# A two-matmul MLP on one Trainium2 core: another order of loads at the start, and other engines for the w2 casts and the plain output copies

## The chip, the cores and the metric

The kernel runs on one core of one Trainium2 chip. The time is device microseconds of one execution. Each kernel is executed several times; a time below is the median with the lowest and the highest in brackets.

Names used below: TensorE is PE in the profile (PEld is its weight load), VectorE is DVE, ScalarE is ACT, GpSimd is POOL, SyncE is SP (the engine that issues most of the loads).

## The reference, cut to what matters

```python
# x: 8 x 1024 x 1024, w1: 1024 x 4096, w2: 4096 x 1024, all float32
h = x @ w1
h = 0.5 * h * (1 + np.tanh(np.sqrt(2 / np.pi) * (h + 0.044715 * h ** 3)))   # gelu
return (h @ w2).astype(np.float32)
```

## The kernel before

The 8192 rows of x are worked on in eight superblocks of 1024 rows. The first matmul is done with 7 block products in place of 8: x and w1 are cut into 2 x 2 blocks, and sums of blocks are multiplied. Inputs are float32 in HBM and are cast to float16 on the chip. The first superblock is special. While it runs, w1 and w2 have to be loaded and cast, and the sums are made. Its second matmul is done plainly, in two column halves (`b = 0` and `b = 1`). The second superblock reloads the cast w1 (`raw_d`), makes the sums again and writes them to HBM (`w1_d`, shown as `w_d_77` to `w_d_80` in the profile: the four quarters of w1). From the third superblock on everything is loaded ready made.

Four engines share the small work. Their queues are worked off in order.

The tile pools. `gc` is the float32 staging for loads of weights (4 buffers), `tmp` is the float32 scratch for block results and output tiles (10 buffers), `u` is for all float16 operands.

```python
    up = ctx.enter_context(tc.tile_pool(name="up", bufs=26))
    gcp = ctx.enter_context(tc.tile_pool(name="gcp", bufs=4))
    tp = ctx.enter_context(tc.tile_pool(name="tp", bufs=10))
    # ... (other pools cut)
    def tt(out, in0, in1, op):                      # L107: every VectorE add or subtract
        nc.vector.tensor_tensor(out=out, in0=in0, in1=in1, op=op)
    # ...
    def pool_copy(out, in_):                        # L118: every GpSimd cast
        pool_last[0] = nc.gpsimd.tensor_copy(out=out, in_=in_)
```

The start. `x_first` loads and transposes both halves of x on TensorE; only then are the first columns of w1 loaded.

```python
        if sb == 0:
            quads.append(MadeQuad(0, True))
            xs.make(5)
            cs = quads[0].load_cols(0, 1)
            quads[0].sum(4, cs)
            for m in (1, 3, 7, 6):
                if m != 3:
                    xs.make(m)
                quads[0].sum(m, cs)
            for c, n in ((1, 1), (2, 2)):
                cs = quads[0].load_cols(c, n)
                for m in SUMS:
                    quads[0].sum(m, cs)
        else:
            for step in range(QC):
                ahead(0, step)                      # second superblock: reload raw w1, make sums, write them
```

The sums of the second superblock go to HBM through GpSimd's queue, and so do the output stores:

```python
        def sum(self, m, sl=slice(None)):
            make_sum(self.ops, m, self.raw, KH, QW, sl)
            if not self.first:
                nc.gpsimd.dma_start(out=w1_d[self.q][:, m - 1, :], in_=flat(self.ops[m]))   # L184
        # ...
        def copy_plain(self):
            for m in PLAIN:
                nc.gpsimd.dma_start(out=w1_d[self.q][:, m - 1, :], in_=flat(self.ops[m]))   # L192
    # ...
    def store(sb, b, q, src):
        # ...
        queue = nc.gpsimd if sb < NSB - 1 else nc.sync
        return queue.dma_start(out=out2[r0:r0 + P, o0:o0 + OH], in_=src)                    # L375
```

The second matmul of the first superblock, with its w2 casts and its output copies:

```python
        for b in range(2):
            # ... (eight PSUM banks; mm() is L395)
            for q in range(NI // QC):
                # ...
                        cast_in(
                            raw[f"{a + 1}{b + 1}"][:, j:j + 2, :],
                            w2v[b, a, :, c:c + 2, :],
                            pool_copy if b == 0 and q < 2 else nc.scalar.copy,
                        )
                # ... (matmuls, sums of w2 and their writes)
            for i in range(2 * NQ):
                for c in range(NI - TAIL, NI):
                    mm(i, c, ready[c])
                o = temp()                                  # a tmp buffer
                if i % 2:
                    nc.scalar.copy(out=o, in_=banks[i])
                else:
                    nc.vector.tensor_copy(out=o, in_=banks[i])      # L443
                last = store(sb, f"{i // NQ + 1}{b + 1}", i % NQ, o)
```

In the first matmul of every superblock, four gelus on ScalarE turn a column's results into the blocks g11, g12, g21, g22 (in the profile of before g_215 to g_218).

## Time and profile before

| | before |
|---|---|
| time | 1606.63 us (1605.54 to 1608.92, 3 runs) |
| profiled run: span, mean granted TensorE clock | 1603.7 us, 0.996 |
| TensorE starts: first real matmul / second superblock / its second matmul | 18.28 / 245.73 / 342.60 us |
| from there to the last matmul | 1256.80 us |

TensorE is busy nearly all the time. From the page of before, the first part (busy us, share of the span, instructions) and the chain of waits (shares of the span by engine, then by line):

```profile
PE 1578.2 (98%) x7296; PEld 717.9 (45%) x7296; DVE 819.6 (51%) x1047; ACT 472.3 (29%) x784; POOL 132.1 (8%) x228
...
PE 95%; DMA 3%; DVE 1%; ACT 1%; issue 0%; SPq 0%; POOL 0%; DVEq 0%
```

A full-width matmul takes 0.216 us at full clock, so what can be gained is the idle time of TensorE. These lines are TensorE's order of time in before: start us, duration us, engine, line, operation, operands, how many; then in brackets the idle time just before the group and what ended it.

```profile
34.33 10.17 PE L277 MATMUL ps<-u 128*128 128x512 f16 x46 [0.18 <-DVE tmp L107]
44.65 71.14 PE L277 MATMUL ps<-u 128*128 128x512 f16 x328
123.20 5.97 PE L277 MATMUL ps<-u 128*128 128x512 f16 x20 [7.41 <-ACT g_216 L287]
...
191.68 0.59 PE L395 MATMUL ps<-u,g_217 128*128 128x512 f16 x1 [3.34 <-DVE tmp L443]
...
245.73 97.03 PE L277 MATMUL ps<-u 128*128 128x512 f16 x448
```

The reader sees two waits, 7.41 us for a gelu on ScalarE before the end of the first stage and 3.34 us for an output copy on VectorE between the two column halves. Before 34.33 us there are smaller gaps. From 245.73 us on, the second superblock's first matmul is one row with no wait.

And up to 246 us the DMA engines had no room: their mean busy share ("DMA share") was 1.00 in the first of these two stretches, and 0.70 in the second. In the view by stretches (stretch, length, then busy us and instructions of PE, PEld, DVE, ACT, POOL, then clock, DMA share, GB/s), before:

```profile
185.60:246.00 60.40, 57.06 (x259) 25.53 (x258) 21.06 (x21) 2.37 (x5) 11.92 (x23) 0.97 1.00 382
246.00:342.70 96.70, 96.70 (x449) 43.80 (x448) 64.15 (x89) 45.88 (x80) 12.21 (x24) 1.00 0.70 218
```

### The profile page before, as it was taken

What the parts mean: (1) busy time and instruction counts of PE and PEld (TensorE: products, weight loads), DVE (VectorE), ACT (ScalarE), POOL (GpSimd) and SP (SyncE); (2) the same over time, 40 slices, a digit from 0 to 9 for tenths busy, and PEclk for the clock granted to TensorE, in tenths of its full rate; (3) what the DMA queues carried; (4) which work ended last, traced back from release to release, by engine and by line L of the source; (5) the groups of instructions that cost most, each with busy time, mean ns of one, the idle gap of its engine ahead of it and who ended that gap; (6) DMA issues with size and microseconds to landing.
All of it is one profiled execution on the core that took longest, in us unless ns stands there. A gap on an engine that the chain in (4) does not pass through costs nothing.

```text
span 1603.7 us, 18985 instructions
## 1 busy us (share of the span) xinstructions
PE 1578.2 (98%) x7296; PEld 717.9 (45%) x7296; DVE 819.6 (51%) x1047; ACT 472.3 (29%) x784; POOL 132.1 (8%) x228
## 2 busy tenths in 40 slices
PE   7989999999999999999999999999999999999999
PEld 4434444444444444444444444444444444444444
DVE  6855336644455444555445554456534555455433
ACT  4645104431044210441114410244103431044310
POOL 2230113001100012000120000100001000000000
PEclk9999999999999999999999999999999999999999
DMA  9999998674566646546574565746557464544511
GB/s 306 345 316 361 276 397 280 179 288 146 197 188 184 236 171 228 157 153 262 186 221 144 169 238 197 227 131 226 201 203 246 102 265 158 210 157 178 216 53 53
DMA packets 161820, 338.91 MB, mean 211 GB/s; under 512 B 72257, under 2 KB 78401, under 8 KB 160833
## 3 DMA queue, kind: packets, MB, share of 16 engines
q1 hardware_dynamic: 146944, 278.97, 50.4%
q0 software_dynamic: 14784, 58.73, 11.5%
q8 instruction: 57, 0.93, 0.2%
q14 instruction: 35, 0.28, 0.1%
HBM read 266.34 MB, written 85.98 MB: 220 GB/s over the span
## 4 chain that ended last, share of the span: by engine, by line
PE 95%; DMA 3%; DVE 1%; ACT 1%; issue 0%; SPq 0%; POOL 0%; DVEq 0%
PE ps L277 46%; PE ps L461 42%; PE ps L395 7%; DMA gc<-in_w_dram 2%; DVE u L107 1%; ACT u L137 0%; DVE tmp L107 0%; DMA u<-in_x_dram 0%; DMA u<-xb 0%; SPq L115 0%; POOL u L118 0%; ACT g_218 L287 0%; ACT g_216 L287 0%; ACT g_217 L287 0%; ACT tmp L343 0%
## 5 line engine op out<-in xcount | busy, mean ns | idle before, releaser
L277 PE MATMUL ps<-u 128*128 128x512 f16 x3584 | 779.8, 380 | 13.1 <-ACT g_216 L287 7.7
L107 DVE TENSOR_TENSOR tmp<-tmp,ps 128x512 f32<-128x512 f32 x652 | 447.1, 687 | 661.6 <-PE ps L461 333.3
L277 PEld LDWEIGHTS <-u 128*128 128x128 f16 x3584 | 351.1, 98 | 440.3 <-issue 15.9
L461 PE MATMUL ps<-u,gc 128*128 128x512 f16 x2240 | 485.7, 379 | 0.0
L461 PEld LDWEIGHTS <-gc 128*128 128x128 bf16 x2240 | 219.2, 98 | 264.3
L375 POOL DMA_DIRECT2D out_dram<-tmp x112 | 60.6, 542 | 1108.0 <-ACT tmp L481 733.9
L107 DVE TENSOR_TENSOR u<-u 128x2048 f16<-128x2048 f16 (+2 forms) x110 | 123.0, 1152 | 56.6 <-ACT u L137 21.5
L343 ACT COPY tmp<-ps 128x512 f32<-128x512 f32 x128 | 73.0, 570 | 258.2 <-PE ps L277 258.2
L107 DVE TENSOR_TENSOR tmp<-ps,tmp 128x512 f32<-128x512 f32 x128 | 88.4, 691 | 5.9 <-PE ps L277 1.2
L481 ACT COPY tmp<-ps 128x512 f32<-128x512 f32 x28 | 16.4, 586 | 177.3 <-PE ps L461 177.3
L395 PE MATMUL ps<-u,g_217 128*128 128x512 f16 x128 | 49.0, 383 | 3.3 <-DVE tmp L443 3.3
L395 PE MATMUL ps<-u,g_218 128*128 128x512 f16 x128 | 49.0, 383 | 0.0
L395 PE MATMUL ps<-u,g_215 128*128 128x512 f16 x128 | 48.9, 382 | 0.0
L395 PE MATMUL ps<-u,g_216 128*128 128x512 f16 x128 | 48.8, 381 | 0.0
L137 ACT CAST u<-gc 128x1024 f16<-128x1024 f32 x36 | 37.2, 1044 | 37.6 <-DMA gc<-in_w_dram 37.6
L487 ACT COPY tmp<-ps 128x512 f32<-128x512 f32 x28 | 16.4, 586 | 80.3 <-PE ps L461 80.3
L475 ACT COPY tmp<-ps 128x512 f32<-128x512 f32 x28 | 16.4, 586 | 74.9 <-PE ps L461 74.9
L118 POOL CAST u<-gc 128x1024 f16<-128x1024 f32 (+1 forms) x26 | 28.5, 1105 | 73.8 <-DMA gc<-in_w_dram 60.0
L254 POOL DMA_DIRECT2D xb<-in_x_dram x56 | 27.5, 509 | 18.1 <-DMA out_dram<-tmp 14.5
L441 ACT COPY tmp<-ps 128x512 f32<-128x512 f32 x8 | 4.7, 586 | 71.1 <-PE ps L395 71.1
L395 PEld LDWEIGHTS <-g_218 128*128 128x128 bf16 x128 | 12.6, 98 | 18.8 <-issue 3.9
L395 PEld LDWEIGHTS <-g_215 128*128 128x128 bf16 x128 | 12.6, 99 | 15.5 <-issue 0.8
(120 smaller groups left out, 848.8 us busy)
## 6 DMA issues: line engine op xcount, KB each, us to landing
gc<-in_w_dram SPq DMA_DIRECT2D x64, 512.0 KB, 6.8
out_dram<-tmp POOLq DMA_DIRECT2D x112, 256.0 KB, 4.4
u<-w_d_85 SPq DMA_DIRECT2D x49, 512.0 KB, 6.4
u<-w_d_86 SPq DMA_DIRECT2D x49, 512.0 KB, 7.1
u<-w_d_87 SPq DMA_DIRECT2D x49, 512.0 KB, 5.8
u<-w_d_88 SPq DMA_DIRECT2D x49, 512.0 KB, 6.3
u<-w_d_77 SPq DMA_DIRECT2D x42, 512.0 KB, 4.8
u<-w_d_78 SPq DMA_DIRECT2D x42, 512.0 KB, 5.1
```

Of the source, the lines that this page charges most:

```text
L107: nc.vector.tensor_tensor(out=out, in0=in0, in1=in1, op=op)
L118: pool_last[0] = nc.gpsimd.tensor_copy(out=out, in_=in_)
L137: cast(out=dst, in_=st)
L254: nc.gpsimd.dma_start(out=xb[q:q + P, :], in_=x2[s * SB + q:s * SB + q + P, :])
L277: nc.tensor.matmul(bank, lhsT=ops[m][:, k, cs], rhs=xs[m][:, k, :], start=(first and k == 0), stop=(k == KH - 1), skip_group_check=not first,)
L343: nc.scalar.copy(out=v, in_=pb)
L375: return queue.dma_start(out=out2[r0:r0 + P, o0:o0 + OH], in_=src)
L395: nc.tensor.matmul(banks[i], lhsT=g[f"{i // NQ + 1}{a + 1}"][:, c, (i % NQ) * P:(i % NQ + 1) * P], rhs=w[a], start=(c == 0 and a == 0), st ...
L461: nc.tensor.matmul(banks[q], lhsT=a[:, c, :], rhs=pieces[c // QC][:, c % QC, :], start=(first and c == 0), stop=(c == NI - 1), skip_group_ ...
L475: nc.scalar.copy(out=v[q], in_=ps)
L481: nc.scalar.copy(out=c21, in_=ps)
L487: nc.scalar.copy(out=c12, in_=ps)
```

## The change

Three parts, with the intent of each.

1. Start: the first two column chunks of w1's first column half are loaded between the two halves of x, in two loads of wider rows, so that the first product can follow the transposes at once.
2. Casts: all w2 casts of the first column half go to GpSimd (before: half of them), and of the second column half only the first two quarters stay on ScalarE.
3. Copies: all plain output copies of the first superblock go to ScalarE, so that none stands behind VectorE's subtractions.

```diff
-        def load_cols(self, c, n):
+        def load_cols(self, c, n, b):
             cs = slice(c * P, (c + n) * P)
-            kn = 2 * KH // n
-            for b in range(2):
-                cast = (nc.scalar.copy, pool_copy)[b]
-                for k in range(2 * KH - kn, -1, -kn):
-                    # ... (loads of kn chunks of rows, cast per half)
+            for a in (1, 0):
+                st = gcp.tile([P, KH, n * P], F32, name="gc")
+                load_in_order(st, w1v[b, :, a * KH:(a + 1) * KH, cs])
+                cast = pool_copy if (a, b) == (0, 1) else nc.scalar.copy
+                cast(out=self.raw[f"{a + 1}{b + 1}"][:, :, cs], in_=st)
             return cs
@@ x_first returns a function half(a) that loads and transposes one half of x @@
@@ start of the first superblock @@
-            quads.append(MadeQuad(0, True))
-            xs.make(5)
-            cs = quads[0].load_cols(0, 1)
-            # ... (sums of chunk 0, then loads and sums of chunk 1 and of chunks 2-3)
+            first = MadeQuad(0, True)
+            quads.append(first)
+            x_half(1)
+            xs.make(2)
+            cs = first.load_cols(0, 2, 0)
+            first.sum(4, cs)
+            x_half(0)
+            xs.make(5, 1)
+            first.load_cols(0, 2, 1)
+            first.sum(1, cs)
+            first.sum(3, cs)
+            for m in (7, 6):
+                xs.make(m)
+                first.sum(m, cs)
+            for b in range(2):
+                cs = first.load_cols(2, 2, b)
+            for m in SUMS:
+                first.sum(m, cs)
@@ w2 casts @@
-                            pool_copy if b == 0 and q < 2 else nc.scalar.copy,
+                            nc.scalar.copy if b == 1 and q < 2 else pool_copy,
@@ output copies of the first superblock @@
-                if i % 2:
-                    nc.scalar.copy(out=o, in_=banks[i])
-                else:
-                    nc.vector.tensor_copy(out=o, in_=banks[i])
+                nc.scalar.copy(out=o, in_=banks[i])
```

More of the change, by code (lines that the diff above doesn't have):

```diff
@@ L163, in load @@
                     )
-        def load_cols(self, c, n):
+        def load_cols(self, c, n, b):
             cs = slice(c * P, (c + n) * P)
-            kn = 2 * KH // n
-            for b in range(2):
-                cast = (nc.scalar.copy, pool_copy)[b]
-                for k in range(2 * KH - kn, -1, -kn):
-                    st = gcp.tile([P, kn, n * P], F32, name="gc")
-                    load_in_order(st, w1v[b, :, k:k + kn, cs])
-                    for a in range(k // KH, (k + kn) // KH):
-                        cast(
-                            out=self.raw[f"{a + 1}{b + 1}"][:, :, cs],
-                            in_=st[:, a * KH - k:(a + 1) * KH - k, :],
-                        )
+            for a in (1, 0):
[3 more added lines that the diff above has]
+                cast(out=self.raw[f"{a + 1}{b + 1}"][:, :, cs], in_=st)
             return cs
@@ L222, in x_first, with half @@
         make_identity(nc, identity)
-        blocks = x_blocks()
-        xs = XOps(blocks)
-        for a in (1, 0):
+        xs = XOps(x_blocks())
+        def half(a):
             for q in range(NQ):
@@ L242, in x_first @@
                     eng(
-                        out=blocks[f"{a + 1}{k + 1}"][:, :, q * P:(q + 1) * P],
+                        out=xs.blocks[f"{a + 1}{k + 1}"][:, :, q * P:(q + 1) * P],
                         in_=ps.rearrange("p (j t) -> p j t", t=P),
                     )
-            if a:
-                xs.make(2)
-        return xs
+        return xs, half
     def x_cast(s, after):
@@ L318, in matmul1 @@
         if sb == 0:
-            quads.append(MadeQuad(0, True))
-            xs.make(5)
-            cs = quads[0].load_cols(0, 1)
-            quads[0].sum(4, cs)
-            for m in (1, 3, 7, 6):
-                if m != 3:
-                    xs.make(m)
-                quads[0].sum(m, cs)
-            for c, n in ((1, 1), (2, 2)):
-                cs = quads[0].load_cols(c, n)
-                for m in SUMS:
-                    quads[0].sum(m, cs)
+            first = MadeQuad(0, True)
[16 more added lines that the diff above has]
+                first.sum(m, cs)
         else:
@@ L503 @@
     nc.scalar.activation(out=warm, in_=warm, func=GELU)
-    xs = x_first()
+    xs, x_half = x_first()
     for sb in range(NSB):
```

## The prediction

> **What bounds it now.** TensorE is busy 98% of the 1603.7 us span and is 95% of the chain of waits. From 245.9 us on the chain is an unbroken row of matmuls (96.7 us per stage), so only the first 246 us can give anything. There the order of time of PE shows three losses:
> 1. Start. The first real matmul starts at 18.3 us, and PE has gaps until 34.3 us. From 18.3 to 44.65 us it does 96 matmuls, which need 20.7 us at the steady 0.216 us: 5.7 us lost, part of it at half clock (0.43 us per matmul).
> 2. End of the first matmul stage. PE idles 7.4 us before 123.2, waiting for the g12 gelu on ScalarE, which stood behind w2 casts whose loads had not landed (ScalarE idle 8.0 us before the cast at 118.8). Then 7 matmuls at 0.43 us: 1.5 us more. About 9 us.
> 3. Between the halves of the second matmul PE idles 3.3 us for a VectorE copy at 190.95 us, behind an x subtraction that waited 7.2 us for a transposing DMA; half clock follows. About 5 us.
>
> DMA is just as full: share 0.96 from 18 to 104 us; 512 KB loads land about 1.3 us apart.
>
> **What the change does.**
> - Start: the instruction order shows PE still doing all 64 transposes before the first product, so the start waits for the last x load (14.6 us before, now behind 1 MB more: about 17.5). Product 4 can follow at once, but VectorE does four x subtractions (1.2 us each) before its first PSUM work. I expect 1-3 us gained. The first column loads (1.75 us each, 512-byte rows) become loads of 1 KB rows (1.45 us), and casts free staging buffers earlier: the DMA stream gets a few us ahead by the end of w1's second quarter (43.05 us before).
> - w2 casts (1.04 us on either engine): all of the first column half move to GpSimd, so loss 2 as it stood goes. But in ScalarE's new order the cast of the second half's first piece stands ahead of the last column's g12 gelu, for which the last product 6 waits. That load landed at 126.35 us; the DMA stream sets it. I estimate 123: cast, gelu, product 6 at about 125 (129.5 before). PE is there at 118, idles 6-7 us, and runs at half clock for some us. So loss 2 is mostly replaced by the same wait one step later: 1.5-4 us gained, the start's gain included.
> - Output copies all on ScalarE (0.59 us against 0.69): nothing stands before them, so loss 3 goes: about 5 us.
>
> The Trainium skill, "TensorE: Matmul & The Clock Gate", Part 1, says that an idle window of about 3.4 us brings the half clock. This trace agrees in kind: 0.43 us per matmul for about 3 us after the 7.4 us wait.
>
> **Prediction.** 1606.6 - 8.5 = 1598 us, 80% range 1591 to 1603. Faster by over 2%: 0.01; within 2%: 0.98; slower: 0.01.
>
> **What would show it.** No VectorE-released PE wait near 185 us; one PE wait of 4-8 us released by the g12 gelu just before the second matmul stage, with ScalarE idle for a w2 load before it; first real matmul near 17 us; later stages still 96.7 us each.
>
> **What would make it wrong.** If the second half's first w2 load lands by 118 us, all of loss 2 goes (about 1590). If VectorE's x subtractions or a cold clock stretch the start, or GpSimd's casts hold the staging buffers, only loss 3's 5 us remain. New waits in the second superblock's start (w1 reloads) could eat those.

## More of the kernel before

GpSimd's order of time in before:

```profile
240.64 0.53 POOL L192 DMA_DIRECT2D w_d_79<-u  x1 [10.89 <-DMA u<-raw_d_83]
243.11 0.53 POOL L192 DMA_DIRECT2D w_d_79<-u  x1 [1.94 <-DMA u<-raw_d_83]
243.63 4.26 POOL L375 DMA_DIRECT2D out_dram<-tmp  x8
```

GpSimd stood 10.89 us at a write of the third w1 quarter, whose reload had not landed, and all eight output stores of the second column half stood behind it until 243.63 us. VectorE, in the same run, already met their late landing:

```profile
253.36 0.69 DVE L107 TENSOR_TENSOR tmp<-tmp,ps 128x512 f32<-128x512 f32 x1 [1.56 <-DMA out_dram<-tmp]
```

VectorE waited 1.56 us for a `tmp` buffer whose store had not landed. It cost TensorE nothing, because TensorE came just late enough.

## The result, and the profile after

| | before | changed |
|---|---|---|
| time | 1606.34 us (1605.54 to 1608.92, 4 runs) | 1606.01 us (1605.34 to 1609.71, 4 runs) |
| ratio, 95% interval | | 1.0 (0.9981 to 1.0019) |
| profiled run: span, clock | 1603.7 us, 0.996 | 1607.9 us, 0.993 |
| TensorE starts: second superblock / its second matmul | 245.73 / 342.60 us | 244.04 / 346.87 us |
| from there to the last matmul | 1256.80 us | 1256.80 us |

The time is the same. One caution: the profiled run of the changed kernel was the slowest of its four (1609.71 us; the other three 1605.34 to 1606.1 us), so the 4.3 us that its second matmul starts later is not a difference of the kernels. Its waits are read below for what they are and where they stand; their typical size is read from the experiments.

The last row of the table is a fixed ruler. In all 19 traces the stretch from the second superblock's second matmul to the last matmul is 1256.80 us. So the whole question is decided before 347 us.

TensorE's order of time in the changed kernel:

```profile
34.16 89.50 PE L271 MATMUL ps<-u 128*128 128x512 f16 x408 [2.93 <-DVE tmp L107]
...
130.53 1.86 PE L271 MATMUL ps<-u 128*128 128x512 f16 x4 [6.44 <-ACT g_102 L281]
...
244.04 4.48 PE L271 MATMUL ps<-u 128*128 128x512 f16 x20
252.38 31.91 PE L271 MATMUL ps<-u 128*128 128x512 f16 x140 [3.86 <-DVE tmp L107]
```

The copy wait between the halves (191.68 us in before) is gone. The gelu wait has moved to the last product of the first stage, as foreseen, and a new wait of 3.86 us stands at the start of the second superblock, with half clock after it (the clock was 0.5 from 251.8 to 255.2 us).

Why the gelu wait is still there, in ScalarE's order of time in the changed kernel:

```profile
121.97 0.60 ACT L281 ACTIVATE g_103<-ps 128x512 bf16<-128x512 f32 x1 [0.37 <-PE ps L271]
128.94 1.04 ACT L137 CAST u<-gc 128x1024 f16<-128x1024 f32 x1 [6.37 <-DMA gc<-in_w_dram]
129.89 0.59 ACT L281 ACTIVATE g_102<-ps 128x512 bf16<-128x512 f32 x1
```

The first w2 cast of the second column half stands ahead of the last column's g12 gelu (g_102). Its load landed at 128.92 us. The Trainium skill, "Perfetto Trace Analysis", in the section on the Tensor Engine instruction, says that ScalarE, VectorE and GpSimd work strictly first in, first out; this trace agrees: TensorE had run out of other work at 124.1 us, and the gelu ran only behind the cast, at 129.89 us.

And the new wait, first on VectorE, then in GpSimd's queue:

```profile
246.02 0.69 DVE L107 TENSOR_TENSOR tmp<-tmp,ps 128x512 f32<-128x512 f32 x1 [0.56 <-PE ps L271]
251.64 1.47 DVE L107 TENSOR_TENSOR tmp<-tmp,ps 128x512 f32<-128x512 f32 x2 [4.92 <-DMA out_dram<-tmp]
```

```profile
242.21 0.53 POOL L186 DMA_DIRECT2D w_d_79<-u  x1 [9.06 <-DMA u<-raw_d_83]
244.70 0.53 POOL L186 DMA_DIRECT2D w_d_79<-u  x1 [1.96 <-DMA u<-raw_d_83]
245.22 3.75 POOL L375 DMA_DIRECT2D out_dram<-tmp  x7
```

VectorE waited for the first output store of the second column half. That store was issued at 245.22 us, behind two writes of the third w1 quarter that had to wait for reloads, and landed at 251.52 us. In before the stores were issued at nearly the same time, 243.63 us. The stretch is as full of transfers as before:

```profile
185.60:246.00 60.40, 60.40 (x282) 27.37 (x281) 18.98 (x16) 7.18 (x13) 11.46 (x22) 1.00 1.03 387
246.00:342.70 96.70, 92.58 (x421) 41.30 (x420) 60.28 (x84) 42.86 (x74) 13.89 (x27) 0.98 0.66 207
```

### The profile page after: what moved, and what is told of

The parts are those of the page before. It is cut to its first block, busy times and chain, and to the rows that moved or that the text cites. A ratio compares the mean times of both kernels' runs of the same rounds, so it can differ in the third digit from the quotient of the medians.

```text
span 1607.9 us, 18982 instructions
## 1 busy us (share of the span) xinstructions
PE 1580.4 (98%) x7296; PEld 720.4 (45%) x7296; DVE 813.3 (51%) x1034; ACT 464.2 (29%) x776; POOL 147.0 (9%) x240
## 4 chain that ended last, share of the span: by engine, by line
PE 88%; DMA 7%; SPq 2%; DVE 1%; POOL 1%; issue 1%; ACT 0%; DVEq 0%; POOLq 0%
PE ps L271 43%; PE ps L458 42%; DMA gc<-in_w_dram 3%; PE ps L395 3%; SPq L115 1%; DMA u<-raw_d_82 1%; DVE u L107 1%; DMA u<-raw_d_83 1%; POOL u L118 1%; DMA u<-in_x_dram 1%; SPq L152 0%; DMA u<-raw_d_84 0%; PE ps L228 0%; DMA out_dram<-tmp 0%; DVE tmp L107 0%
## 5 line engine op out<-in xcount | busy, mean ns | idle before, releaser
L107 DVE TENSOR_TENSOR u<-u 128x2048 f16<-128x2048 f16 (+1 forms) x105 | 121.0, 1184 | 80.0 <-POOL u L118 20.0
L343 ACT COPY tmp<-ps 128x512 f32<-128x512 f32 x128 | 73.0, 570 | 258.5 <-PE ps L271 258.1
L478 ACT COPY tmp<-ps 128x512 f32<-128x512 f32 x28 | 16.4, 587 | 177.3 <-PE ps L458 177.3
L118 POOL CAST u<-gc 128x1024 f16<-128x1024 f32 x38 | 42.9, 1140 | 126.3 <-DMA gc<-in_w_dram 115.6
L484 ACT COPY tmp<-ps 128x512 f32<-128x512 f32 x28 | 16.4, 586 | 80.3 <-PE ps L458 80.3
L472 ACT COPY tmp<-ps 128x512 f32<-128x512 f32 x28 | 16.4, 586 | 74.9 <-PE ps L458 74.9
L440 ACT COPY tmp<-ps 128x512 f32<-128x512 f32 x16 | 9.4, 586 | 91.7 <-PE ps L395 90.3
L137 ACT CAST u<-gc 128x1024 f16<-128x1024 f32 x20 | 20.9, 1043 | 18.8 <-DMA gc<-in_w_dram 16.6
L228 PE MATMUL ps<-identity,u 128*128 128x128 f32 x64 | 12.7, 386 | 7.8 <-DMA u<-in_x_dram 7.8
L395 PEld LDWEIGHTS <-g_101 128*128 128x128 bf16 x128 | 12.7, 99 | 15.6 <-issue 0.8
```

The costliest lines, as they stand in the source:

```text
L137: cast(out=dst, in_=st)
L343: nc.scalar.copy(out=v, in_=pb)
L395: nc.tensor.matmul(banks[i], lhsT=g[f"{i // NQ + 1}{a + 1}"][:, c, (i % NQ) * P:(i % NQ + 1) * P], rhs=w[a], start=(c == 0 and a == 0), st ...
L472: nc.scalar.copy(out=v[q], in_=ps)
L478: nc.scalar.copy(out=c21, in_=ps)
L484: nc.scalar.copy(out=c12, in_=ps)
```

## The experiments

Theory A: time gained early is given back at the start of the second superblock, where VectorE waits for `tmp` buffers whose output stores stand in GpSimd's queue behind w1 writes. Theory B: the changed start loses what the copies win. Theory C: the DMA stream as a whole holds that stretch, and buffers and queues don't matter. (The expectations of e1 to e4: each says itself what its A and B stand for.) Seventeen kernels ran, all with correct results. "Arrival" below is TensorE's first matmul of the second superblock, "second matmul" the start of that superblock's second matmul, to which 1256.80 us and the head and tail of the span are added.

| run | arrival | longest wait just after it | second matmul | time, median | ratio to before |
|---|---|---|---|---|---|
| before | 245.73 | none | 342.60 | 1606.01 / 1608.05 / 1605.65 / 1606.82 (the four series) | |
| e1_start | 243.32 | 1.81 | 342.81 | 1605.22 | 0.9997 (0.9983 to 1.0012) |
| e2_casts | 233.26 | 9.14 | 342.76 | 1605.32 | 0.9997 (0.9982 to 1.0012) |
| e3_copies | 241.44 | 3.55 | 344.69 | 1606.95 | 1.0006 (0.999 to 1.0023) |
| e4_casts_copies | 231.43 | 11.09 | 342.08 | 1604.38 | 0.9987 (0.9972 to 1.0002) |
| e6_store_act | 244.52 | 2.54 | 344.09 | 1606.26 | 0.9991 (0.9978 to 1.0004) |
| e8_after_store_act | 248.25 | 1.72 | 347.00 | 1611.38 | 1.0021 (1.0008 to 1.0034) |
| e9_after_pool_store | 248.34 | 1.01 | 346.38 | 1608.08 | 1.0005 (0.9993 to 1.0016) |
| e11_start_no_gpsimd | 243.42 | 3.06 | 345.17 | 1607.86 | 0.9998 (0.9986 to 1.001) |
| e12_store_b1 | 231.78 | 4.13, then 3.96 | 340.35 | 1603.31 | 0.9978 (0.9965 to 0.9991) |
| e13_after_store_b1 | 241.99 | 1.50 | 340.52 | 1604.78 | 0.9996 (0.9978 to 1.0014) |
| e14_after_pool_store_b1 | 231.85 | 3.93 | 334.61 | 1599.94 | 0.9964 (0.995 to 0.9979) |
| e15_start_no_gpsimd | 230.86 | 4.61 | 335.49 | 1598.39 | 0.9952 (0.994 to 0.9965) |
| e16_after_gc_out | 243.04 | 0.53 | 340.94 | 1601.77 | 0.9968 (0.9955 to 0.998) |
| e17_after_pool_gc_out | 232.20 | 2.75 | 334.63 | 1597.55 | 0.9943 (0.993 to 0.9955) |
| e18_pool_gc_out | 230.93 | 6.69 | 336.26 | 1600.06 | 0.9962 (0.9948 to 0.9975) |
| e19_after_pool | 232.83 | 2.87, then 6.90 | 341.50 | 1605.03 | 0.999 (0.9978 to 1.0003) |
| e20_scalar_start_gc_out | 230.31 | 4.16 | 334.15 | 1596.35 | 0.9934 (0.9916 to 0.9952) |

The rows e1 to e4 ran with the first series of before, e6 to e11 with the second, e12 to e15 with the third, e16 to e20 with the fourth (e20 later).

### The parts one by one: e1 to e4

**e1_start**: before with part 1 alone (the changed kernel with these lines put back).

```diff
-                            nc.scalar.copy if b == 1 and q < 2 else pool_copy,
+                            pool_copy if b == 0 and q < 2 else nc.scalar.copy,
-                nc.scalar.copy(out=o, in_=banks[i])
+                if i % 2:
+                    nc.scalar.copy(out=o, in_=banks[i])
+                else:
+                    nc.vector.tensor_copy(out=o, in_=banks[i])
```

Expected:

> The kernel before with the start part alone (half of w1's first columns between the two halves of x); w2 casts and output copies as before. Theory A (the change is several parts of opposite sign: the start part makes PE reach steady matmuls about 4 us later than before, because VectorE's x subtractions, a slow GpSimd cast and a half-clock stretch stand in its way): 1606 to 1610 us, first gapless matmul row from about 34 us with only about 36 matmuls done there (50 before). Theory B (the start part gains 1 to 3 us as predicted, and the loss is elsewhere): 1603 to 1605 us.

**e2_casts**: before with part 2 alone.

```diff
-                            pool_copy if b == 0 and q < 2 else nc.scalar.copy,
+                            nc.scalar.copy if b == 1 and q < 2 else pool_copy,
```

Expected:

> The kernel before with the move of the w2 casts alone. In its instruction order ScalarE has the last g12 gelu ahead of the first cast of the second half, so the 7.4 us wait before the second matmul should be gone and PE should enter it near 122 us (130.3 before). Theory A (gains made early are given back at a later point that the DMA stream sets): VectorE's output copy still stands behind the x subtraction that waits for the transposing DMA until about 190 us, so PE waits there some 10 us instead of 3.3, and the time is 1604 to 1607 us. Theory B (each wait is independent): 1597 us, 9 us less than before.

**e3_copies**: before with part 3 alone.

```diff
-                if i % 2:
-                    nc.scalar.copy(out=o, in_=banks[i])
-                else:
-                    nc.vector.tensor_copy(out=o, in_=banks[i])
+                nc.scalar.copy(out=o, in_=banks[i])
```

Expected:

> The kernel before with all output copies of the first superblock on ScalarE, nothing else. The 3.3 us wait between the halves of the second matmul goes in both theories. Theory A: PE arrives at the second superblock some 5 us earlier (241 instead of 246) and there waits for tmp buffers, whose stores are issued by GpSimd only after w1 writes that wait for reloads (issued at 243.6 us before): 1603 to 1607 us with a new PE wait of 3 to 6 us near 245 to 252 us. Theory B: 1601 us, no new wait.

**e4_casts_copies**: before with parts 2 and 3 (both edits above), so the change without its start.

Expected:

> The change without its start part: w2 casts mostly on GpSimd and all output copies on ScalarE. Both waits of the first superblock should be gone in both theories, so PE arrives at the second superblock near 232 us. Theory A (a cap there: tmp buffers whose stores stand in GpSimd's queue behind w1 writes that wait for DMA): a PE wait of 10 us or more near 236 to 252 us, and 1603 to 1607 us in all. Theory B (no cap; the start part ate the gain): about 1592 us.

Measured: no part alone moves the time beyond its interval. The times of e2, e3 and e4 lie in their ranges for theory A, that of e1 between its two ranges. The 10 us wait between the halves that was expected for e2 did not come (1.84 us there); its long wait, 9.14 us, stands at the second superblock. Yet the waits that the parts for casts and copies aim at do go. In e2 and e4 there is no wait before the second matmul, in e3 and e4 none between the halves. TensorE's order of time in e4:

```profile
120.92 110.67 PE L395 MATMUL ps<-u,g 128*128 128x512 f16 x512
231.43 4.48 PE L277 MATMUL ps<-u 128*128 128x512 f16 x20
247.00 95.25 PE L277 MATMUL ps<-u 128*128 128x512 f16 x428 [11.09 <-DVE tmp L107]
342.08 6.21 PE L458 MATMUL ps<-u,g 128*128 128x512 f16 x28
```

The whole second matmul of the first superblock is one row of 512 matmuls, TensorE arrives 14.3 us earlier than in before, does 20 matmuls, and then waits 11.09 us. The clock was 0.5 from 238.5 to 252.2 us, so the matmuls from 247.00 to 252.2 us ran at half speed, about 2.6 us more. Of 14.3 us, 0.5 us is left at the second matmul. In the four runs TensorE arrives anywhere from 231.4 to 243.3 us and goes on after its wait at 246.9 to 249.6 us. In e4 the first output store of the second half was issued at 236.06 us and landed at 246.13 us; VectorE went on at 246.25 us. (The instruction records in the packed trace show what this issue had waited for: a semaphore, a counter that tells of a transfer's landing. A w1 write eight transfers earlier in GpSimd's queue still held it, and landed at 235.51 us.) That is what theory A says, and it refutes theory B as the main cause: e4 has the old start and gains as little. It does not yet tell A from C, because a store that takes 10 us to land is also a sign of a full DMA stream.

### The stores on ScalarE's queue, all of the first superblock: e6, e8, e9, e11

```diff
-        queue = nc.gpsimd if sb < NSB - 1 else nc.sync
+        queue = nc.scalar if sb == 0 else nc.gpsimd if sb < NSB - 1 else nc.sync
```

**e6_store_act** is e4 with this edit. Expected:

> The change without its start part, and with the first superblock's output stores issued from ScalarE's queue (right after each copy) instead of GpSimd's, so that they no longer stand behind w1 writes there. PE's instructions are the same as without the move of the stores. Theory A (the gain is given back only at the tmp buffers, which wait for stores stuck in GpSimd's queue): the wait near 236 to 247 us (11.1 us) is gone or under 3 us, and the time falls to 1590 to 1596 us. Theory C (the DMA stream as a whole is the bound until about 250 us, whatever the queues): another wait for DMA takes its place and the time stays at 1602 to 1606 us.

**e8_after_store_act** is the changed kernel with it. Expected:

> The whole change plus the same move of the first superblock's stores to ScalarE's queue. Theory A: the wait at the second superblock's start (3.9 us and half clock after it) is gone; the wait of 6.4 us for the g12 gelu and the start part's loss stay and are now seen in the time: 1599 to 1603 us. Theory C: 1604 to 1607 us.

**e9_after_pool_store** is e8 with all w2 casts on GpSimd:

```diff
-                            nc.scalar.copy if b == 1 and q < 2 else pool_copy,
+                            pool_copy,
```

Expected:

> The whole change, the stores on ScalarE's queue, and all w2 casts on GpSimd, so that no w2 cast stands ahead of the last g12 gelu on ScalarE. Theory A: the 6.4 us wait before the second matmul goes as well, and what is left against the kernel without the start part is the start part's own cost, 2 to 5 us: 1593 to 1598 us. If the start part cost nothing, it would equal that kernel (1590 to 1596). Theory C: 1602 to 1606 us.

**e11_start_no_gpsimd** is e9 with all early casts of w1's first columns on ScalarE:

```diff
-                cast = pool_copy if (a, b) == (0, 1) else nc.scalar.copy
+                cast = nc.scalar.copy
```

Expected:

> As the run before, with the two casts of w1's first columns that were on GpSimd (one of them took 3.3 us while VectorE worked) moved to ScalarE. If the slow GpSimd cast is what delays the start part, PE's gapless row begins some 2 us earlier, with more matmuls done, and the time is 1 to 2 us lower than in the run before; if VectorE's x subtractions are the limit, it is the same within 1 us.

Measured: e6, e8 and e9 missed the ranges of both theories, and e11 came within 0.3 us of e9, so there the casts on GpSimd made no difference that shows. None is faster than before, e8 is 0.2% slower. The trace shows that the edit did two things besides the one intended. First, the copy of x for the third superblock (`xb`) hangs on the last of these stores and on GpSimd's queue; with no store ahead of it there, it ran among the w2 casts. GpSimd in e6:

```profile
120.82 1.04 POOL L118 CAST u<-gc 128x1024 f16<-128x1024 f32 x1 [8.74 <-DMA gc<-in_w_dram]
121.81 0.97 POOL L254 DMA_DIRECT2D xb<-in_x_dram  x2
```

In before these copies are issued from 248.41 us on. This put 8 extra loads into a full stream: the transposing loads of x were done at 200.9 us (189.5 in before), and the first reload of raw w1 was issued at 215.0 us (203.0). Second, ScalarE now stood in its own store issues between the halves, and TensorE with it; e6:

```profile
182.33 1.01 PE L395 MATMUL ps<-u,g 128*128 128x512 f16 x2 [4.06 <-ACT tmp L440]
```

So these runs can't tell the theories apart. They do show that the queue of a store is part of the timing of everything behind it.

### Only the second half's stores, without the last: e12 to e15

The last store stays on GpSimd, so that the x copies behind it stay where they were.

```diff
-        queue = nc.gpsimd if sb < NSB - 1 else nc.sync
+        late_half = sb == 0 and b[1] == "2" and (b, q) != ("22", NQ - 1)
+        queue = nc.scalar if late_half else nc.gpsimd if sb < NSB - 1 else nc.sync
```

**e12_store_b1** is e4 with this edit. Expected:

> The change without its start part, and the output stores of the second column half of the first superblock, except the last one, issued from ScalarE's queue instead of GpSimd's (the last stays, so that the x copies that hang on it stay where they are). Theory A (the gain is given back at the start of the second superblock, because VectorE waits for tmp buffers whose stores stand in GpSimd's in-order queue behind w1 writes): the tmp wait near 247 us goes or falls under 3 us, TensorE starts the superblock near 231-233 us, and the time is 1591 to 1597 us. Theory C (the DMA stream as a whole bounds this stretch, and the queue does not matter): another wait of about the same length turns up at 240-252 us, and the time stays at 1602 to 1606 us.

**e13_after_store_b1** is the changed kernel with it. Expected:

> The changed kernel with the same store edit. Theory A: the tmp wait of 3.9 us near 252 us goes, the 6.4 us gelu wait before the second matmul and the slower start stay, so 1599 to 1603 us. Theory C: 1604 to 1608 us, a wait remains at the start of the second superblock.

**e14_after_pool_store_b1** is e13 with all w2 casts on GpSimd (the edit of e9). Expected:

> The changed kernel with the same store edit and all w2 casts on GpSimd. The 6.4 us gelu wait goes. If the start part itself costs time, it is 1 to 5 us above the run without the start part of the same call, with the first gapless matmuls having done fewer products by 34 us; if it costs nothing, the two are within 1 us. Theory C again: 1604 to 1608 us.

**e15_start_no_gpsimd** is e14 with the early w1 casts on ScalarE (the edit of e11). Expected:

> As the run before it, with the two early casts of w1's first columns on ScalarE instead of GpSimd. If GpSimd's slow cast (3.3 us in the changed kernel) costs the start, 0.5 to 2 us faster than the run before it; if not, the same within 0.5 us.

Measured: e12, e14 and e15 are faster than before by 0.2 to 0.5%, outside their intervals; e13 is not. For e12, e13 and e14 the numbers of theory A did not come out: e12's 1603.31 us and e13's 1604.78 us lie in the ranges of theory C, and e14 is 3.4 us below e12, where 1 to 5 us above it or the same was expected. e15 is 1.5 us below e14, as expected if the early GpSimd casts cost something, but the two intervals overlap. The trace of e12 shows what was left. Seven stores were issued from 223.59 us on and the first landed at 230.78 us, in place of 246.13 us in e4. But the eighth, left on GpSimd, was issued at 244.34 us and landed at 254.52 us, and VectorE came to its buffer. In e13 the seven stores were issued promptly, 233.74 to 241.51 us, and still landed at 240.82 to 253.15 us. (Its trace, with a longest wait of 1.50 us, is of one of its faster runs, 1603.49 us; no trace shows what its slower ones, up to 1609.88 us, did.) So part of the wait is the landing time itself. The Trainium skill, "DMA: Bandwidth & Descriptors", section "Issuing engines are not separate DMA queues", says that transfers of all issuing engines run on the same 16 DMA engines and interleave; these runs agree: in e14 the eight stores of this half, seven of them from ScalarE's queue, took 6.9 to 13.1 us (median 9.3 us) to land, at a DMA share of 1.05 from 222 to 252 us.

There was a third cost. ScalarE in e14 (ACTq lines are its DMA issues):

```profile
229.46 0.59 ACT L441 COPY tmp<-ps 128x512 f32<-128x512 f32 x1 [0.71 <-PE ps L396]
233.80 0.34 ACTq L376 DMA_DIRECT2D out_dram<-tmp  x1
234.23 0.59 ACT L441 COPY tmp<-ps 128x512 f32<-128x512 f32 x1 [4.19 <-PE ps L271]
236.97 0.34 ACTq L376 DMA_DIRECT2D out_dram<-tmp  x1
237.41 0.59 ACT L441 COPY tmp<-ps 128x512 f32<-128x512 f32 x1 [2.59 <-DMA u<-raw_d]
```

The sixth copy was done at 230.05 us, its store was issued only at 233.80 us, and the seventh store at 236.97 us; the profile puts the last wait down to a reload of raw w1, which landed at 236.90 us. TensorE waited 3.93 us for ScalarE there. The instruction records of the trace tell by what means a store on ScalarE waited for a load of SyncE. This program counts the landings of all its transfers on 16 semaphores, eight for SyncE and ScalarE in common and eight for GpSimd. The sixth and the seventh store each waited for the one on which a SyncE reload was still to land (233.72 and 236.90 us), and then used it themselves. The store issues of e6 between the halves waited in the same way, one of them for a w2 load that landed at 181.23 us. So moving the stores to ScalarE tied them to the reloads by the program's own bookkeeping.

### Other buffers, queues untouched: e16 to e19

This takes away what makes VectorE wait, the `tmp` buffers, and leaves every queue alone. During the second half's copies the four `gc` staging buffers are free (the last w2 load has landed near 170 us), so the eight output tiles go there, two to a buffer.

```diff
-                o = temp()
+                if b == 0:
+                    o = temp()
+                else:
+                    if i % 2 == 0:
+                        pair = gcp.tile([P, 2, HT], F32, name="gc")
+                    o = pair[:, i % 2, :]
                 nc.scalar.copy(out=o, in_=banks[i])
```

**e16_after_gc_out** is the changed kernel with this edit alone. Expected:

> The changed kernel with one edit: the eight output copies of the second column half of the first superblock go to staging buffers of the w loads (free at that time) in place of tmp buffers; the stores stay in GpSimd's queue. If the wait at 252 us is for tmp buffers and nothing else ends at the same time, it goes: no VectorE wait on the output stores in 240-262 us, the second superblock's second matmul starts at 340 to 341.5 us (346.9 in the changed kernel), time 1600 to 1604 us. If the DMA stream itself holds VectorE (reloads of raw w1), a PE wait of 3 us or more stays at 244-254 us and the time is 1604 to 1607 us.

**e17_after_pool_gc_out** is e16 with all w2 casts on GpSimd (the edit of e9). Expected:

> The run before with all w2 casts on GpSimd, so without the gelu wait before the second matmul. TensorE gets to the second superblock near 231.5 us. If tmp buffers were the cap: at most 4 us of waits there (VectorE's sum waits for a reload of raw w1 that landed at 236.9 us in the run with the stores on ScalarE), second superblock's second matmul at 328.5 to 333 us, time 1592 to 1598 us. If the DMA stream is the cap: a wait of 6 us or more, time 1599 to 1604 us.

**e18_pool_gc_out** is e17 with the start of before. Expected:

> The run before with the start of the kernel before in place of the changed start. If the changed start gains (a DMA stream some 3 to 5 us ahead, read at the reloads of raw w1 near 200 us): 1 to 4 us slower than the run before. If it loses: 1 to 3 us faster. If it does nothing: within 0.7 us.

**e19_after_pool** is the changed kernel with all w2 casts on GpSimd and nothing else. Expected:

> The changed kernel with all w2 casts on GpSimd and nothing else: the 6.4 us gelu wait before the second matmul goes, and TensorE gets to the second superblock 8 to 12 us earlier. If the start of the second superblock has the cap: TensorE resumes there at 246 to 252 us all the same after a tmp wait of 8 us or more, time 1603 to 1606.5 us. If there is no cap, 1594 to 1599 us.

Measured: e16 is 0.32% faster than before, where the changed kernel is even. Its TensorE lines:

```profile
131.06 112.15 PE L395 MATMUL ps<-u,g 128*128 128x512 f16 x510
243.04 33.92 PE L271 MATMUL ps<-u 128*128 128x512 f16 x156
277.50 1.02 PE L271 MATMUL ps<-u 128*128 128x512 f16 x4 [0.53 <-DVE tmp L107]
```

The wait at 252 us is gone, and no other took its place: 156 matmuls in a row from the arrival. The stores themselves were as late as in the changed kernel (the first was issued at 244.15 us and landed at 250.46 us). So the first half of theory A, that the held `tmp` buffers cost the time, is shown for the changed kernel. Its second half, that the stores land late because of their place in GpSimd's queue, is read from the traces; the runs that moved the stores (e6 to e15) did not show it alone. The gelu wait before the second matmul is still there (8.33 us in this run).

e19 and e17 make the pair that shows the cap alone. Both have all w2 casts on GpSimd, both are free of the gelu wait, both arrive near 232.5 us. Both times lie in the ranges that were expected if the buffers are the cap; e17's second matmul, at 334.63 us, came later than the 328.5 to 333 us expected. TensorE's order of time, first e19, then e17:

```profile
232.83 3.62 PE L271 MATMUL ps<-u 128*128 128x512 f16 x16
239.31 1.04 PE L271 MATMUL ps<-u 128*128 128x512 f16 x4 [2.87 <-DVE tmp L107]
247.25 94.41 PE L271 MATMUL ps<-u 128*128 128x512 f16 x428 [6.90 <-DVE tmp L107]
```

```profile
232.20 3.62 PE L271 MATMUL ps<-u 128*128 128x512 f16 x16
238.56 32.05 PE L271 MATMUL ps<-u 128*128 128x512 f16 x140 [2.75 <-DVE tmp L107]
```

With `tmp` buffers, 11.2 us of earlier arrival (against 244.04 us of the changed kernel) end at 1605.03 us, within the interval of no change. With other buffers the 6.90 us wait goes, and the time is 1597.55 us, 0.57% under before.

What is left in e17 is a small share of theory C. VectorE's sum at 236.69 us waited 9.51 us for a reload of raw w1, and its PSUM work stood behind that sum; this is the 2.75 us wait. e18, with the old start, has no such wait there, and a longer one later:

```profile
230.93 33.92 PE L277 MATMUL ps<-u 128*128 128x512 f16 x156
271.54 64.88 PE L277 MATMUL ps<-u 128*128 128x512 f16 x292 [6.69 <-DVE tmp L107]
```

There VectorE waited 8.91 us, to 269.07 us, for a reload of the fourth w1 quarter. e17 met the same reload, with less to wait, because TensorE came later. VectorE's lines, first e17, then e18:

```profile
268.72 1.23 DVE L107 TENSOR_TENSOR u<-u 128x2048 f16<-128x2048 f16 x1 [2.79 <-DMA u<-raw_d]
269.07 1.23 DVE L107 TENSOR_TENSOR u<-u 128x2048 f16<-128x2048 f16 x1 [8.91 <-DMA u<-raw_d]
```

So once the buffers are out of the way, the DMA stream does set the pace: the next cap is that reload. e15 and e20 met it too (VectorE went on at 269.58 and 268.24 us).

e17 and e18 differ in the start alone. By their medians the changed start gains 2.5 us (1597.55 against 1600.06, as expected if it gains; the two intervals just overlap). It does not gain on TensorE: TensorE reaches the second matmul at 121.69 us in e17, at 120.43 us in e18, 1.3 us later. The DMA stream is ahead for a while: the transposing loads of x are done at 187.9 us in e17 and at 190.6 us in e18. But at the reload of the fourth quarter 0.35 us of that is left. In the two traces the second matmul starts 1.63 us apart, and half clock accounts for most of it: after its wait of 6.69 us e18 ran its matmuls from 271.54 to 274.83 us at half speed, about 1.6 us more, while e17's half clock (238.40 to 241.81 us) fell before the wait for that reload, which took it up. So the gain is likely, but how it comes about is not shown.

### The version that the runs point to: e20

**e20_scalar_start_gc_out** is e17 with the early w1 casts on ScalarE (the edit of e11). Expected:

> The version that the runs point to: the changed kernel with all w2 casts on GpSimd, the two early casts of w1's first columns on ScalarE, and the second half's output copies in free staging buffers. TensorE gets to the second superblock near 231 us, waits of at most 4 us there, second superblock's second matmul at 333 to 335 us; time 1595 to 1598 us, the ratio to the kernel before 0.993 to 0.995. If GpSimd's early casts cost nothing, it is the same as with them on GpSimd (1597.6 us in the call before) within 0.7 us.

Measured: 1596.35 us (1592.77 to 1602.11, 6 runs), ratio 0.9934 (0.9916 to 0.9952). It beats before by about 10 us, and the changed kernel, which was even with before in its own rounds, by about as much. It is the fastest version, though not clearly apart from e17: TensorE arrives 1.9 us earlier than in e17, and 0.5 us of it is left at the second matmul, behind the reload just named.

The trace shows what the GpSimd casts cost the start. VectorE's row of sums before its first PSUM work, first in e17 (casts on GpSimd at 20.48, 26.44 and 29.48 us), then in e20 (none on GpSimd before 29.48 us):

```profile
19.56 12.57 DVE L107 TENSOR_TENSOR u<-u 128x2048 f16<-128x2048 f16 x13
```

```profile
19.56 10.05 DVE L107 TENSOR_TENSOR u<-u 128x2048 f16<-128x2048 f16 x13
```

The same 13 sums took 2.5 us longer. Three of them are the difference: those that began beside a GpSimd cast took 2.06 us in place of 1.22, and twice 1.52 in place of 0.68. The Trainium skill, "SBUF — State Buffer", section "Who interferes with whom", says that a VectorE instruction with two SBUF inputs contends with a GpSimd instruction that reads SBUF, and that the port pair the two share is an exclusive lock. The trace agrees: each time VectorE lost 0.84 us, most of the 1.04 us that such a cast usually takes. Over all runs the same is seen in the matmuls done by 34 us: 50 to 55 in the seven traces with the old start, 36 to 45 in the nine with the changed start, 45 to 52 in the three with the changed start and ScalarE casts.

## Why the prediction was wrong

The prediction said 1598 us, in a range of 1591 to 1603 us. It is 1606.01 us.

- **Right: the ceiling.** That "only the first 246 us can give anything" is nearly so: from 342.60 us on nothing moved in any run. But the limit is not 246 us. The second superblock's start belongs to the part that decides.
- **Wrong, and the step that failed: that gains before 245.9 us carry through.** The sum 1606.6 - 8.5 took it that TensorE's row from 245.9 us on would begin earlier by what was gained. The runs showed a cap there: VectorE needs `tmp` buffers whose output stores stand behind w1 writes in GpSimd's queue, and the first of these stores lands only at 246 to 252 us. e4 arrived 14.3 us earlier and kept 0.5 us; e19 arrived 12.9 us earlier and kept 1.1 us at the second matmul. With that wait taken away by other buffers and nothing else touched, the changed kernel is 0.32% faster than before (e16, about 5 us). So about 5 us of the expected 8.5 us were given back at this place. The prediction named "New waits in the second superblock's start (w1 reloads)" as a way to be wrong, and gave it no weight in its number. The place was right; but in the changed kernel VectorE's wait there ended with an output store, not with a reload.
- **Right in mechanism, wrong in size: the gelu wait.** It did move one step later, behind the first w2 cast of the second half, as the order of instructions showed. But the load was put at 123 us, because the stream was to be ahead, and landed at 128.92 us in the changed kernel's profile (126.35 us in before; 126.6 to 127.8 us in e8, e13 and e16, which have the same start and casts), and product 6 ran at 130.53 us in place of "about 125". So the term "1.5-4 us gained, the start's gain included" was not there. That the casts left on ScalarE do this is shown by e16 against e17, which differ in them alone: 8.33 us of wait or none, 1601.77 us or 1597.55 us.
- **Wrong sign on TensorE, partly right on DMA: the start.** "I expect 1-3 us gained" did not come for TensorE, which did fewer matmuls by 34 us in every run with the changed start and GpSimd casts. VectorE did 13 sums in a row (12.57 us in e17) before its first PSUM work for a product, not four, and three of them ran into GpSimd casts. In the changed kernel's profile the first product came at 20.28 us, not "near 17 us", behind a gap of 3.42 us in the transposes and half clock after it. That "the DMA stream gets a few us ahead by the end of w1's second quarter" did not come there: that load landed at 44.19 us in the changed kernel (43.05 in before) and at 41.5 us in e17 (42.0 in e18). Later it did come with all w2 casts on GpSimd: with the changed start the transposing loads were done at 186.2 to 188.5 us (e14, e15, e17, e19, e20; not in e9 and e11, where the early `xb` copies delayed them), against 190.6 us in e18. With casts left on ScalarE it did not: 193.1, 189.8 and 191.1 us in the changed kernel, e13 and e16, against 189.5 us in before.
- **Right: the copies.** The wait between the halves went in every run with the copies on ScalarE and its stores on GpSimd. Its gain was eaten by the same cap (e3: arrival 4.3 us earlier, then a 3.55 us wait and half clock).
- **Right: the clock.** The prediction cited the Trainium skill, "TensorE: Matmul & The Clock Gate", Part 1, for half clock after an idle window of about 3.4 us. The records of every run show windows in whole multiples of 3.4 us (3.4, 6.8, 10.2). After the wait in e4 it cost a further 2.6 us. But a shorter wait was enough in e17: after 2.75 us without a matmul the clock was 0.5 from 238.40 to 241.81 us.

How much of the 3.5 us between the 5 us of e16 and the predicted 8.5 us belongs to the start and how much to the later load is not separated by a run. Also open is by what way the changed start gains in e17 against e18.

## What to carry to other kernels

A row of matmuls without a wait is not proof of slack behind it: before counting a gain, look at the engines next to it at the place where the gain would arrive, for waits that today cost nothing (here VectorE's 1.56 us for an output store at 253 us, and GpSimd's 10.89 us in front of the stores). A buffer is held until its store lands, so a store in an in-order queue behind something slow, on a full DMA stream, ties up scratch for much longer than the store itself takes; by the medians, giving such tiles other free buffers was worth more (e16 against e13, e17 against e14) than moving the store to another queue, which moved other things too. A cast moved to an idle engine isn't free if the engine shares a port with a busy one (0.84 us for each early cast in e17).

## What the Trainium skill lacked or had wrong

- "TensorE: Matmul & The Clock Gate", Part 4, says that the full clock doesn't engage for transposes. Here it did: in before the clock was granted in full from 10.2 us, while TensorE had done only float32 transposes, and the 34 transposes measured in that window followed each other every 0.109 us (median), against 0.213 us before it. In the changed kernel's trace, 27 transposes at a granted 0.5 took 0.213 us each again.
- "DMA: Bandwidth & Descriptors", section "Issuing engines are not separate DMA queues", says that issuing from several engines saves only the issue time. It doesn't say that an engine's place in its own queue can decide more: output stores issued from ScalarE began at 223.59 us (e12) and from GpSimd, behind waiting writes, at 236.06 us (e4).
- No page that was used here gives the landing time of a plain store on a full DMA stream. Here a 256 KB store took 6.9 to 13.1 us from issue to landing (e14), at a DMA share of 1.05.
